# The opening of a two-layer decoder trunk: zeros on TensorE, transfers in another order, the first norm moved

## The chip, the core and the metric

The kernel runs on one core of a Trainium2 chip. The metric is the device time of one execution in microseconds (us). Before the change it is 2430.84 us, the median of 3 runs (2429.31 to 2431.43). The core's engines are TensorE (PE, with PEld for its weight loads), VectorE (DVE), ScalarE (ACT), GpSimd (POOL) and SyncE (SP); here SP issues nearly all DMA transfers.

## What is computed

Two decoder layers over a sequence of 256 positions with a model width of 2048, all in float32, then a last norm. Cut to what matters:

```python
for i in range(2):
    a = rmsnorm(h, attn_norm[i])
    h = h + mixer_i(a)               # q, k, v projection, attention over 16 heads, w_out
    h = h + conv_ffn(rmsnorm(h, ffn_norm[i]), w_up[i], conv_w[i], conv_b[i], w_down[i])
    gate = sigmoid(rmsnorm(h, ple_norm[i]) @ w_ple_gate[i])
    h = h + gate * (p[i] @ w_ple[i])
return rmsnorm(h, final_norm)
```

`p[i] @ w_ple[i]` depends on an input alone. In layer 0 the kernel computes it first of all, before the first projection of the mixer.

## The kernel before

**Tiling.** Activations lie with features on the 128 partitions: `h` is 128 x 16 x 256, feature block by position. All products of weights go through `gemm_unit` (L196). A *unit* is a piece of weights, 128 x (kc blocks of 128 rows) x 256 columns; 4 blocks in most places, 2 for `w_ple`. Every float32 weight piece `wr` is split in two rounded parts: ACT casts the high part (`split_unit`, L165), DVE subtracts it to get the low part (L166). Activations are split likewise into `act` (for the first norm in `norm_parts`, L269 on ACT and L271 on DVE, straight from `h`, since the row factor of the norm is multiplied in behind the product). Three products (high x high, high x low, low x high, `PARTS`) of 128 x 128 by 128 x 256 make up one block, so a unit of 4 blocks is 24 matmuls and one of `w_ple` 12. PE cannot do more than the first two matmuls of a unit before DVE has delivered its low part.

**Order.** The program is written by one Python pass. `tick()` counts units on PE; `defer(n, fn)` puts work n units later. A scheduling layer then fixes one order for each engine. `unit` keeps 3 split units ahead; there are 4 buffers `w` for split weights and 3 buffers `wr` of 8 KB per partition for raw ones. Transfers of weights are *groups*: the first two of 256 KB, then five of 512 KB up to the first w_in pieces, later 1 MB (`_groups`, L90). Below, g0 to g4 are the groups of `w_ple` (8 units), g5 to g8 the four units of the first q product `psq`, g9 and on the units of `psk`; x0 to x3 are the four 512 KB pieces of `h`.

**The opening.** SP issues, in this order, `pr` (the input p), g0, g1, x0, g2, x1, then g3, g4, x2, g5, x3, g6 and the constants `ct`. From g3 on a group has to wait for the split of the group that held its buffer `wr`, and what stands behind it on SP waits as well. POOL issues the gains `gn`, and then `posi`, `bft` and `cv`. PE works through 8 units `psp` (p times w_ple, whose results ACT copies to `pl`), 4 of `psq`, 4 of `psk`, 4 of `psv`, and so on with the next pair of heads. The first norm's sum of squares is made on the way: `norm_squares` (ACT L281, DVE adds to `acc` L282) for all 8 pieces of `h` two units behind the last `psp`, `norm_sums` (four tiny matmuls `nps`, then some 13 operations of two columns on DVE) at 3 units and `norm_rows` (two matmuls `rps`, which give the row factors `rb` and `rq`) at 5 units behind, which is within `psk`.

**Layout.** Pools are allocated in the order `cpool` (h, the activation buffers act0 and act1, pact, pl, constants), `wpool` (wr, w), `work`.

```python
PARTS = ((0, 0), (0, 1), (1, 0))
room = 512 if i < 2 else 1024 if i < 12 else 2048
LOOK = 3
```

Of the kernel before, what the change touches and what calls it, by code (L numbers as in the profile page):

```python
# [17 lines left out]
P = 128  # L18
# [86 lines left out]
def trunk(ctx: ExitStack, tc: tile.TileContext, xT, pT, pos, gains, conv, bf, cst, wst, out):  # L105
    nc = tc.nc

    cpool = ctx.enter_context(tc.tile_pool(name="cpool", bufs=1))
    wpool = ctx.enter_context(tc.tile_pool(name="wpool", bufs=1))
    work = ctx.enter_context(tc.tile_pool(name="work", bufs=1))  # L110
    psum = ctx.enter_context(tc.tile_pool(name="psum", bufs=1, space=bass.MemoryType.PSUM))

    h = cpool.tile([P, KT, S], F32, name="h")
    bufs = [cpool.tile([P, KT, 2, S], F32R, name=f"act{i}") for i in range(2)]
    pact = cpool.tile([P, 2, 2, S], F32R, name="pact")
    pl = cpool.tile([P, KT, S], F32, name="pl")
    gn = cpool.tile([P, 7, KT], F32, name="gn")
    cv = cpool.tile([P, DEPTH, 2 * FT, 4], F32, name="cv")
# [12 lines left out]
    def at_tile(name):  # L131
        return psum.tile([P, 2, 512], F32, name=name, tag="at", bufs=2)
# [11 lines left out]
    def issue_group():  # L144
        g = GROUPS[at["group"]]
        n = sum(u[3] * u[5] for u in g)
        raw = wpool.tile([P, 2048], F32, name="wr", tag="wr", bufs=3)
        src = wst[at["off"]:at["off"] + P * n].rearrange("(p f) -> p f", p=P)
        nc.sync.dma_start(out=raw[:, :n], in_=src)
        at["off"] += P * n  # L150
        at["group"] += 1
        o = 0
        for u in g:
            m = u[3] * u[5]
            raws.append((u, raw[:, o:o + m].rearrange("p (k c) -> p k c", c=u[5])))
            o += m
# [25 lines left out]
    def defer(n, fn):  # L182
        later.append((at["tick"] + n, fn))
# [125 lines left out]
    def norm_rows(mixer):  # L309

        dg = t2_tile("nd", (P, 2, P))
        ps = at_tile("rps")
        for t in range(2):
            nc.vector.tensor_scalar_mul(out=dg[:, t, :], in0=ident, scalar1=rT[:, t:t + 1])
            if mixer is None:
                nc.tensor.matmul(ps[:, 0, t * P:(t + 1) * P], lhsT=ones, rhs=dg[:, t, :],
                                 start=t == 0, stop=True, skip_group_check=True)
        if mixer is None:
            return ps[:, 0, :S]
        dh, dl = t2_tile("ndh", (P, 2, P), F32R), t2_tile("ndl", (P, 2, P), F32R)  # L320
        nc.scalar.copy(out=dh, in_=dg)
        nc.vector.tensor_sub(out=dl, in0=dg, in1=dh.bitcast(F32))
        for i, x in enumerate((dh, dl)):
            nc.tensor.matmul(ps[:, 0, :S], lhsT=trir[:, 0, :], rhs=x, start=i == 0, stop=i == 1)
        nc.vector.tensor_copy(out=rb, in_=ps[:, 0, :S])
        if mixer:
            nc.vector.tensor_scalar_mul(out=rq, in0=rb, scalar1=SCALE)

    def norm_finish(mixer):
        at["rows"] = at["tick"] + 5  # L330
        defer(3, norm_sums)
        defer(5, lambda: norm_rows(mixer))

    def with_rows(fn):

# [14 lines left out]
    def ple_up(l, op):  # L350

        ps = mm_tile("psp")
        gemm(ps, pact, "w_ple", l, op * 256, (2,))
        nc.scalar.copy(out=pl[:, 2 * op:2 * op + 2, :], in_=ps)

    def load_x(i):
        nc.sync.dma_start(out=h[:, 4 * i:4 * i + 4, :], in_=xT[:, 4 * i:4 * i + 4, :])

    nc.gpsimd.dma_start(out=gn, in_=gains)
    praw = load_p(0)  # L360
    issue_group()
    issue_group()
    load_x(0)
    issue_group()
    nc.vector.tensor_copy(out=pact[:, :, 0, :], in_=praw)
    nc.vector.tensor_sub(out=pact[:, :, 1, :], in0=praw, in1=pact[:, :, 0, :].bitcast(F32))
    load_x(1)
    bft = cpool.tile([P, NH], F32, name="bft")
    posi = cpool.tile([32, S], I32, name="posi")
    trir = cpool.tile([P, 2, P], F32R, name="trir")  # L370

    def rest_of_start():
        issue_group()
        issue_group()
        load_x(2)
        issue_group()
        load_x(3)
        issue_group()

    def constants():  # L380
        nc.sync.dma_start(out=ct, in_=cst)
        nc.vector.tensor_copy(out=trir, in_=ct[:, C_ONE:C_ONE + 256].rearrange("p (a b) -> p a b", a=2))
        nc.gpsimd.dma_start(out=posi, in_=pos)
        nc.gpsimd.dma_start(out=bft, in_=bf)
        nc.gpsimd.dma_start(out=cv, in_=conv)


    rc = cpool.tile([32, S], F32, name="rc")
# [179 lines left out]
    def head_pair(l, hp, act, dst, st):  # L568
# [13 lines left out]
        with_rows(lambda ps=ps: nc.vector.tensor_mul(out=q, in0=ps, in1=rq2))  # L582
        ps = mm_tile("psk")
        gemm(ps, act, "w_in", l, D + hp * 256, full)
        nc.vector.tensor_mul(out=k, in0=ps, in1=rb2)

        def first():
            if l % 2 == 0 and hp < 4:
# [10 lines left out]
        if l % 2 == 0 and hp >= 4:  # L599
            rope(q)  # L600
            rope(k)
        defer(2 + (l % 2 == 0 and hp >= 4), first)
        if l % 2 == 1 and hp == 0:
            return
        ps = mm_tile("psv")
# [32 lines left out]
    for l in range(DEPTH):  # L638
        st = {}
        if l == 0:  # L640
            split_unit()
            rest_of_start()
            for op in range(8):
                ple_up(0, op)
            for i in range(8):
                norm_parts(i, 0, X)
            constants()

            def squares():
                for i in range(8):  # L650
                    norm_squares(i)

            defer(2, squares)
            norm_finish(True)
        for hp in range(NH // 2):
            head_pair(l, hp, X, Y, st)
            if l > 0:
# [161 lines left out]
```

## Time and profile before

| | |
|---|---|
| median of 3 runs | 2430.84 us |
| the profiled execution, its own time | 2430.3 us |
| its span, first to last instruction | 2428.5 us |
| mean granted TensorE clock | 0.997 |
| DVE, ACT busy | 66%, 51% of the span |
| moved by DMA | 458.06 MB, mean 189 GB/s |

The 1.8 us between the span and the execution's own time lie outside of all instructions. The profile's page gives busy time and a chain that is followed back from the last instruction; the timeline lists the instructions of one engine in order of time, alike neighbours merged: start, duration, engine, line, operation, written tile <- read tiles, count, and in brackets the idle time ahead and what ended it. The times of a merged row run to the end of the last instruction, so the next row may start before that: instructions overlap at their ends.

### The profile page before, as it was taken

The page shows a single profiled execution, that of the slowest core. Times are in us where ns is not written, and L with a number is a line of the kernel's source. Part 1 is how long each engine was busy: PE and PEld are TensorE (multiplying, and loading weights), DVE is VectorE, ACT ScalarE, POOL GpSimd, SP SyncE. Part 2 cuts the span into 40 slices and gives each one's busy share as a digit, 9 for nine tenths or more (in the row PEclk, how much of TensorE's full clock was granted, in tenths as well). Part 3 has the DMA queues.
Part 4 walks back from the last instruction along what each step waited for, and adds up shares of the span by engine and source line. Part 5 has one row for each costly group of instructions (what it writes and reads, how often), then busy time and mean ns, then how long its engine had stood idle before and what let it go on. Part 6 is the DMA issues. An engine that isn't in the chain of part 4 may idle for free.

```text
span 2428.5 us, 47969 instructions
## 1 busy us (share of the span) xinstructions
PE 2406.8 (99%) x20974; PEld 2400.7 (99%) x20974; DVE 1595.8 (66%) x2157; ACT 1228.6 (51%) x1549; POOL 2.5 (0%) x8
## 2 busy tenths in 40 slices
PE   8999999999999999999999999999999999999997
PEld 8999999999999999999999999999999999999997
DVE  7557666776567657767765555667665776667676
ACT  6554455554355445555554444555544554455553
POOL 0000000000000000000000000000000000000000
PEclk9999999999999999999999999999999999999998
DMA  7444445555555555555455445555555555555553
GB/s 269 174 174 174 170 178 191 192 195 198 197 191 191 187 200 196 197 185 204 176 184 181 170 170 167 199 191 198 193 191 192 193 198 191 201 191 187 193 196 120
DMA packets 66484, 458.06 MB, mean 189 GB/s; under 512 B 7409, under 2 KB 7425, under 8 KB 16609
## 3 DMA queue, kind: packets, MB, share of 16 engines
q1 hardware_dynamic: 66096, 454.53, 53.0%
q8 instruction: 164, 2.69, 0.4%
q0 software_dynamic: 176, 0.46, 0.1%
q14 instruction: 48, 0.39, 0.0%
HBM read 452.86 MB, written 2.10 MB: 187 GB/s over the span
## 4 chain that ended last, share of the span: by engine, by line
PE 98%; DVE 1%; DMA 1%; issue 0%; ACT 0%; SPq 0%; DVEq 0%; ACTq 0%
PE psu L203 39%; PE psd L203 20%; PE pso L203 7%; PE psk L203 7%; PE psq L203 7%; PE psv L237 7%; PE psg L203 7%; DMA wr<-in_w 1%; PE avp L518 1%; PE psp L203 0%; PE pse L717 0%; PE scs L474 0%; PE psv L250 0%; PE sps L509 0%; PE avp L520 0%
## 5 line engine op out<-in xcount | busy, mean ns | idle before, releaser
L166 DVE TENSOR_TENSOR w<-wr,w 128x1024 fp32r<-128x1024 f32 (+2 forms) x882 | 1051.9, 1193 | 694.4 <-ACT w L165 686.8
L165 ACT CAST w<-wr 128x1024 fp32r<-128x1024 f32 (+2 forms) x882 | 905.4, 1028 | 1080.4 <-PE psu L203 353.5
L203 PE MATMUL psu<-act,w 128*128 128x256 f32 x8448 | 959.3, 276 | 0.0
L203 PEld LDWEIGHTS psu<-act,w 128*128 128x128 f32 x8448 | 958.3, 188 | 0.0
L203 PE MATMUL psd<-act,w 128*128 128x256 f32 x4224 | 479.7, 276 | 0.0
L203 PEld LDWEIGHTS psd<-act,w 128*128 128x128 f32 x4224 | 479.2, 188 | 0.0
L203 PE MATMUL psq<-act,w 128*128 128x256 f32 x1536 | 185.7, 280 | 1.2 <-DVE w L166 1.2
L203 PEld LDWEIGHTS psq<-act,w 128*128 128x128 f32 x1536 | 180.3, 188 | 1.8 <-DVE w L166 1.6
L203 PE MATMUL psk<-act,w 128*128 128x256 f32 x1536 | 179.8, 277 | 0.0
L203 PEld LDWEIGHTS psk<-act,w 128*128 128x128 f32 x1536 | 176.5, 188 | 0.0
L203 PE MATMUL pso<-act,w 128*128 128x256 f32 x1536 | 175.8, 277 | 0.0
L203 PEld LDWEIGHTS pso<-act,w 128*128 128x128 f32 x1536 | 174.9, 188 | 0.0
L237 PE MATMUL psv<-w,act 128*128 128x256 f32 x1440 | 173.3, 279 | 0.0
L237 PEld LDWEIGHTS psv<-w,act 128*128 128x128 f32 x1440 | 169.0, 188 | 0.6
L203 PE MATMUL psg<-act,w 128*128 128x256 f32 x1440 | 164.4, 276 | 0.0
L203 PEld LDWEIGHTS psg<-act,w 128*128 128x128 f32 x1440 | 163.7, 188 | 0.0
L617 DVE TENSOR_TENSOR u<-psu,rb 128x512 f32<-128x512 f32 x88 | 60.9, 692 | 33.3 <-PE psu L203 33.2
L623 DVE SCALAR_TENSOR_TENSOR yv<-u,cv,yv 128x256 f32<-128x256 f32 x176 | 73.4, 480 | 0.0
L623 DVE SCALAR_TENSOR_TENSOR yg<-u,cv,yg 128x256 f32<-128x256 f32 x176 | 73.4, 480 | 0.0
L620 ACT ACTIVATE yg<-u,cv 128x256 f32<-128x256 f32 x88 | 48.1, 594 | 1.0 <-DVE u L617 1.0
L620 ACT ACTIVATE yv<-u,cv 128x256 f32<-128x256 f32 x88 | 48.1, 594 | 0.0
L261 ACT CAST act<-yg 128x512 fp32r<-128x512 f32 x44 | 27.4, 622 | 39.2 <-DVE yg L633 39.2
(172 smaller groups left out, 881.7 us busy)
## 6 DMA issues: line engine op xcount, KB each, us to landing
wr<-in_w SPq DMA_DIRECT2D x388, 1024.0 KB, 4.8
wr<-in_w SPq DMA_DIRECT2D x36, 768.0 KB, 4.3
wr<-in_w SPq DMA_DIRECT2D x8, 896.0 KB, 4.7
wr<-in_w SPq DMA_DIRECT2D x7, 512.0 KB, 6.4
h<-in_x SPq DMA_DIRECT2D x4, 512.0 KB, 6.8
out_dram<-h SPq DMA_DIRECT2D x8, 256.0 KB, 2.4
wr<-in_w SPq DMA_DIRECT2D x2, 816.0 KB, 4.4
ct<-in_c SPq DMA_DIRECT2D x1, 841.0 KB, 7.8
```

The lines of the kernel that those rows point to most:

```text
L165: nc.scalar.copy(out=w[:, :, 0, :], in_=raw)
L166: nc.vector.tensor_sub(out=w[:, :, 1, :], in0=raw, in1=w[:, :, 0, :].bitcast(F32))
L203: nc.tensor.matmul(ps[:, j, :], lhsT=w[:, k, s, js], rhs=act[:, k0 - koff + k, t, :], start=first and j + k + n == 0, stop=last and k == k ...
L237: nc.tensor.matmul(ps[:, t], lhsT=act[:, 4 * i + k, a, tsl], rhs=w[:, k, b], start=i + t + k + n == 0, stop=i == 3 and k == kc - 1 and n = ...
L261: nc.scalar.copy(out=dst[:, :, 0, :], in_=src)
L518: nc.tensor.matmul(av[:, 0, j * S:(j + 1) * S], lhsT=v[:, 0, js], rhs=w[:, j * S:(j + 1) * S], start=j == 0, stop=False, skip_group_check= ...
L617: nc.vector.tensor_mul(out=u[:, :, 2:], in0=ps, in1=rb2)
L620: nc.scalar.activation(out=y[:, j, :], in_=u[:, j, 2:], func=AF.Identity, bias=cv[:, l, t, 3:4], scale=cv[:, l, t, 2:3])
L623: nc.vector.scalar_tensor_tensor(out=y[:, j, :], in0=u[:, j, tap:tap + S], scalar=cv[:, l, t, tap:tap + 1], in1=y[:, j, :], op0=ALU.mult, ...
```

## The change

Six things change.

1. PE starts with 20 matmuls of zeros into a PSUM tile `idle` that nobody reads. Their operand is a part of act1 that DVE clears.
2. The raw `w_ple` groups of layer 0 no longer pass through the `wr` buffers; they are loaded into the tile `pl`, each to the place where its own result is written later.
3. SP issues `pr`, g0, g1, g2, x0, g3, x1, g4, x2, g5, g6, x3, g7, `ct`, and then `posi`, `bft` and `cv`, which POOL issued before.
4. The split of `h` (`norm_parts`) is placed between the units of `psp`, and every second copy of a `psp` result goes to DVE.
5. The squares come one piece per unit (3 to 10 units behind the last `psp`, as the program is written), `norm_sums` at 12 and `norm_rows` at 14 units instead of 3 and 5. The products of q and k with the row factors, and the first attention step, wait for that.
6. The pools are allocated with act0, act1, pact and a gap of 64 bytes first, then the weights' buffers, then the rest. From the sizes of the tiles, `w` lies 130,624 bytes behind act0 before and 69,696 bytes behind it now; both are 64 more than a multiple of 512.

```diff
+    apool = ctx.enter_context(tc.tile_pool(name="apool", bufs=1))
+    wpool = ctx.enter_context(tc.tile_pool(name="wpool", bufs=1))
     cpool = ctx.enter_context(tc.tile_pool(name="cpool", bufs=1))
-    wpool = ctx.enter_context(tc.tile_pool(name="wpool", bufs=1))
...
+    bufs = [apool.tile([P, KT, 2, S], F32R, name=f"act{i}") for i in range(2)]
+    pact = apool.tile([P, 2, 2, S], F32R, name="pact")
+    apool.tile([P, 16], F32, name="gap")
     h = cpool.tile([P, KT, S], F32, name="h")
-    bufs = [cpool.tile([P, KT, 2, S], F32R, name=f"act{i}") for i in range(2)]
-    pact = cpool.tile([P, 2, 2, S], F32R, name="pact")
...
-        raw = wpool.tile([P, 2048], F32, name="wr", tag="wr", bufs=3)
+        if g[0][:2] == ("w_ple", 0):
+            op = g[0][4] // 256
+            raw = pl[:, 2 * op:2 * (op + len(g)), :].rearrange("p a s -> p (a s)")
+        else:
+            raw = wpool.tile([P, 2048], F32, name="wr", tag="wr", bufs=3)
...
-    def norm_finish(mixer):
-        at["rows"] = at["tick"] + 5
-        defer(3, norm_sums)
-        defer(5, lambda: norm_rows(mixer))
+    def norm_finish(mixer, sums=3, rows=5):
+        at["rows"] = at["tick"] + rows
+        defer(sums, norm_sums)
+        defer(rows, lambda: norm_rows(mixer))
...
-        nc.scalar.copy(out=pl[:, 2 * op:2 * op + 2, :], in_=ps)
+        if l == 0 and op % 2 == 1:
+            nc.vector.tensor_copy(out=pl[:, 2 * op:2 * op + 2, :], in_=ps)
+        else:
+            nc.scalar.copy(out=pl[:, 2 * op:2 * op + 2, :], in_=ps)
...
+    zero = bufs[1][:, 0, 0, :]
+    nc.vector.memset(zero.bitcast(F32), 0.0)
+    idle = at_tile("idle")
+    for i in range(20):
+        nc.tensor.matmul(idle[:, 0, :S], lhsT=zero[:, 0:P], rhs=zero, start=True, stop=True)
     nc.gpsimd.dma_start(out=gn, in_=gains)
     praw = load_p(0)
-    issue_group()
-    issue_group()
-    load_x(0)
-    issue_group()
+    for _ in range(3):
+        issue_group()
...
-    load_x(1)
...
     def rest_of_start():
+        load_x(0)
         issue_group()
+        load_x(1)
         issue_group()
         load_x(2)
         issue_group()
+        issue_group()
         load_x(3)
         issue_group()
...
-        nc.gpsimd.dma_start(out=posi, in_=pos)
-        nc.gpsimd.dma_start(out=bft, in_=bf)
-        nc.gpsimd.dma_start(out=cv, in_=conv)
+        nc.sync.dma_start(out=posi, in_=pos)
+        nc.sync.dma_start(out=bft, in_=bf)
+        nc.sync.dma_start(out=cv, in_=conv)
...
-        nc.vector.tensor_mul(out=k, in0=ps, in1=rb2)
+        with_rows(lambda ps=ps: nc.vector.tensor_mul(out=k, in0=ps, in1=rb2))
+        late = max(0, at["rows"] - at["tick"])
...
-        defer(2 + (l % 2 == 0 and hp >= 4), first)
+        defer(2 + late + (l % 2 == 0 and hp >= 4), first)
...
             for op in range(8):
+                if op in (2, 4, 6):
+                    for i in (op - 2, op - 1):
+                        norm_parts(i, 0, X)
                 ple_up(0, op)
+            defer(1, lambda: norm_parts(6, 0, X))
+            defer(2, lambda: norm_parts(7, 0, X))
+            constants()
             for i in range(8):
-                norm_parts(i, 0, X)
-            constants()
-            def squares():
-                for i in range(8):
-                    norm_squares(i)
-            defer(2, squares)
-            norm_finish(True)
+                defer(3 + i, lambda i=i: norm_squares(i))
+            norm_finish(True, 12, 14)
```

How the scheduling layer orders this on an engine is not to be read from the diff. On SP, the start before: `pr`, then weights (`wr`) and pieces of `h` in turn, up to the constants.

```order
L347 DMA pr<-in_p 128x512
L149 DMA wr<-in_w 128x512 x2
L357 DMA h<-in_x 128x1024
L149 DMA wr<-in_w 128x1024
L357 DMA h<-in_x 128x1024
L149 DMA wr<-in_w 128x1024 x2
L357 DMA h<-in_x 128x1024
L149 DMA wr<-in_w 128x1024
L357 DMA h<-in_x 128x1024
L149 DMA wr<-in_w 128x1024
L381 DMA ct<-in_c 128x1682
```

And now (line numbers of the changed kernel are higher by 8 to 18):

```order
L157 DMA pl<-in_w 128x512 x2
L157 DMA pl<-in_w 128x1024
L368 DMA h<-in_x 128x1024
L157 DMA pl<-in_w 128x1024
L368 DMA h<-in_x 128x1024
L157 DMA pl<-in_w 128x1024
L368 DMA h<-in_x 128x1024
L157 DMA wr<-in_w 128x1024 x2
L368 DMA h<-in_x 128x1024
L157 DMA wr<-in_w 128x1024
L399 DMA ct<-in_c 128x1682
L401 DMA posi<-in_pos 32x256
```

The first piece of `h` stands behind g2 instead of ahead of it, and all five groups of `w_ple` have a home of their own. On DVE, before, the place from the last parts of `h` to the sum of the squares; `w<-wr,w` is the low part of a unit, `acc<-acc,sq` an addition of squares:

```order
L271 SCALAR_TENSOR_TENSOR act_68<-h,gn,act_68 128x256 x4
L382 CAST trir<-ct 128x256
L282 TENSOR_TENSOR acc<-acc,sq 128x512
L531 CAST sel_13740<-ct 128x16
L282 TENSOR_TENSOR acc<-acc,sq 128x512
L166 TENSOR_TENSOR w<-wr,w 128x4x256
L282 TENSOR_TENSOR acc<-acc,sq 128x512 x2
L166 TENSOR_TENSOR w<-wr,w 128x4x256
L282 TENSOR_TENSOR acc<-acc,sq 128x512 x2
L166 TENSOR_TENSOR w<-wr,w 128x4x256
L282 TENSOR_TENSOR acc<-acc,sq 128x512
```

And the same place now; the three units `w` ahead of the additions are g5, g6 and g7, the one behind them is g8, the last unit of `psq`:

```order
L174 TENSOR_TENSOR w<-wr,w 128x4x256 x2
L363 COPY pl<-psp 128x512
L279 SCALAR_TENSOR_TENSOR act_70<-h,gn,act_70 128x256 x3
L174 TENSOR_TENSOR w<-wr,w 128x4x256
L279 SCALAR_TENSOR_TENSOR act_70<-h,gn,act_70 128x256
L400 CAST trir<-ct 128x256
L290 TENSOR_TENSOR acc<-acc,sq 128x512
L549 CAST sel_13761<-ct 128x16
L290 TENSOR_TENSOR acc<-acc,sq 128x512 x6
L174 TENSOR_TENSOR w<-wr,w 128x4x256
L295 TENSOR_TENSOR acc<-acc 128x256
```

Before, the splits of units stand between the additions; now all seven additions stand ahead of the split of g8. On ACT it is likewise: seven squares in a row between the casts of g7 and g8. On PE, before, from `psp` to the first attention scores `scs`:

```order
L203 MATMUL psp<-pact,w 128x256 x96
L203 MATMUL psq<-act_68,w 128x256 x96
L203 MATMUL psk<-act_68,w 128x256 x12
L291 MATMUL nps<-ct,acc 128x2 x2
L203 MATMUL psk<-act_68,w 128x256 x50
L324 MATMUL rps<-ndh,trir 128x256
L203 MATMUL psk<-act_68,w 128x256 x8
L324 MATMUL rps<-ndl,trir 128x256
L203 MATMUL psk<-act_68,w 128x256 x26
L237 MATMUL psv<-w,act_68 128x256 x48
L428 MATMUL scs<-q,k 128x256 x2
```

And now:

```order
L375 MATMUL idle<-act_71 128x256 x20
L211 MATMUL psp<-pact,w 128x256 x96
L211 MATMUL psq<-act_70,w 128x256 x96
L211 MATMUL psk<-act_70,w 128x256 x96
L245 MATMUL psv<-w,act_70 128x256 x96
L299 MATMUL nps<-ct,acc 128x2 x2
L211 MATMUL psq<-act_70,w 128x256 x48
L332 MATMUL rps<-ndh,trir 128x256
L332 MATMUL rps<-ndl,trir 128x256
L211 MATMUL psq<-act_70,w 128x256 x48
L446 MATMUL scs<-q,k 128x256 x2
```

The norm's matmuls have left `psk` and stand behind `psv` and in the middle of the next pair's `psq`; the first scores follow one unit group later.

## Prediction, made before the changed kernel had run

> **What bounds the kernel now.** First the page: the busy time by engine and the chain that ended last.
>
> ```profile
> PE 2406.8 (99%) x20974; PEld 2400.7 (99%) x20974; DVE 1595.8 (66%) x2157; ACT 1228.6 (51%) x1549; POOL 2.5 (0%) x8
> ...
> PE 98%; DVE 1%; DMA 1%; issue 0%; ACT 0%; SPq 0%; DVEq 0%; ACTq 0%
> ```
>
> PE is the bound; 21.7 us of the span of 2428.5 are without a matmul. A change of the opening can win only what PE loses there, so I look next at PE's timeline, where it starts and where it stops (idle time in brackets), up to the first `psv`.
>
> ```profile
> 5.87 0.80 PE L203 MATMUL psp<-pact,w 128*128 128x256 f32 x2 [5.87 <-ACT w L165]
> 7.42 13.57 PE L203 MATMUL psp<-pact,w 128*128 128x256 f32 x94 [0.76 <-ACT w L165]
> ...
> 24.27 3.31 PE L203 MATMUL psq<-act,w 128*128 128x256 f32 x24 [0.23 <-DVE w L166]
> 28.59 5.50 PE L203 MATMUL psq<-act,w 128*128 128x256 f32 x46 [1.01 <-DVE w L166]
> 33.93 1.52 PE L203 MATMUL psk<-act,w 128*128 128x256 f32 x12
> ...
> 46.65 5.61 PE L237 MATMUL psv<-w,act 128*128 128x256 f32 x48
> ```
>
> The last wait that counts ends at **28.59**: DVE's low part of g7, the third unit of `psq`. From there PE only runs, apart from the norm's matmuls within `psk`. What was lost ahead of 28.59 (the late start, a slow stretch) cannot be won by itself; whatever lets PE be earlier before that point only makes it wait longer there. So the question is what the last such wait of the changed kernel is, and when it ends.
>
> The pace of PE, from the chain of waits in order of time (start, duration) and from windows (length, PE busy, count, granted clock, DMA share, GB/s):
>
> ```profile
> 59.22 8.48 PE psq L203 x72
> 404.76 8.16 PE psu L203 x72
> 1237.40 10.88 PE psk L203 x96
> ...
> 8.00:12.00 4.00, 4.00 (x21) 1.00 1.02 417
> 13.00:17.00 4.00, 4.00 (x36) 1.00 1.01 371
> ```
>
> 8.16/72 and 10.88/96 give 113.3 ns per matmul, the normal pace; 8.48/72 = 117.8 ns is a second one, seen in some stretches around attention. From 8 to 12 us PE is never idle, yet only 21 matmuls fall into 4 us against 36 from 13 to 17: the start runs at about half pace. The 1.00 in the clock's column there says nothing against it; it may be that no change of clock had been recorded yet.
>
> **The change, part by part.** *Zeros.* 20 matmuls at half pace, about 4/20 = 0.2 us each by the window row of 8 to 12, take some 4 us. The first real matmul needs `pr` and g0 and cannot be before 5.87 as now, so zeros that start by 1.8 cost nothing, and what they may save is the slow stretch: the 22 matmuls of the first two units, which now end at about 12 us, would end at 7.4 + 22 x 0.118 = 10.0. By the paragraph above that is worth something only if it moves the last wait.
>
> *Transfers.* Where do the pieces arrive? ACT's timeline, whose first brackets tell the arrival of x0 (8.4) and of g2 (10.44), and which has the durations for what follows; then the transfers' rates by window, and the transfer of `cv` (median us to landing last).
>
> ```profile
> 8.48 1.71 ACT L269 ACTIVATE act<-h,gn 128x256 fp32r<-128x256 f32 x4 [1.12 <-DMA h<-in_x]
> 10.46 1.14 ACT L165 CAST w<-wr 128x512 fp32r<-128x512 f32 x2 [0.27 <-DMA wr<-in_w]
> ...
> 12.50 0.91 ACT L269 ACTIVATE act<-h,gn 128x256 fp32r<-128x256 f32 x2
> 13.31 0.57 ACT L354 COPY pl<-psp 128x512 f32<-128x512 f32 x1
> 13.78 1.15 ACT L165 CAST w<-wr 128x512 fp32r<-128x512 f32 x2
> 14.82 0.59 ACT L354 COPY pl<-psp 128x512 f32<-128x512 f32 x1
> ...
> 18.50 1.05 ACT L165 CAST w<-wr 128x1024 fp32r<-128x1024 f32 x1
> 19.44 0.60 ACT L354 COPY pl<-psp 128x512 f32<-128x512 f32 x1
> ...
> 24.95 1.14 ACT L281 ACTIVATE sq<-h 128x512 f32<-128x512 f32 x2
> 25.99 1.04 ACT L165 CAST w<-wr 128x1024 fp32r<-128x1024 f32 x1
> ...
> 8.00:14.00 6.00, 1.00 1.02 414
> 14.00:24.00 10.00, 1.00 0.99 353
> ...
> cv<-in_conv POOLq DMA_DIRECT2D x1, 352.0 KB, 7.9
> ```
>
> x0 now stands behind g2, so it comes where g2 came, 10.44, less the time of `cv`, which no longer lies in between: 352 KB at 414 GB/s is 0.9 us, nearly all of it ahead of 10.44. I take **x0 at 9.5** (bounds: 8.4, where it was, and 10.44). Behind it each piece of 512 KB takes 1.3 to 1.5 us (414 to 353 GB/s), so x3, the fifth piece after g3, x1, g4, x2, g5, g6, lands at 9.5 + 7 x 1.4 = 19.3 and g7 at 20.7. In the queue of SP the three small transfers now stand ahead of g8: `ct`, 841 KB, `cv`, 352 KB, and g8 take 4.5 to 5 us, so g8 comes at about 25.5.
>
> *ACT.* From x0 on ACT has work without a pause. From start to start: a pair of `act` 0.81 (12.50 to 13.31), a copy 0.47 (13.31 to 13.78), a pair of small casts 1.04 (13.78 to 14.82), a large cast 0.94 (18.50 to 19.44), a square 0.52 (1.04 for two). Up to the end of the cast of g7 stand 8 such pairs, 4 copies (the other 4 are DVE's now), 2 pairs of small casts, 3 large casts and one square: 6.48 + 1.88 + 2.08 + 2.82 + 0.52 = 13.8, with 0.1 for the tail of the last: 9.5 + 13.9 = **23.4**. Of that end the large cast takes 1.05 and four `act` on x3 1.62, so x3 is needed at 20.7 and g7 at 22.3; both have come. So here ACT decides, not the transfers.
>
> *DVE.* Its rows:
>
> ```profile
> 9.03 1.68 DVE L271 SCALAR_TENSOR_TENSOR act<-h,gn,act 128x256 fp32r<-128x256 f32 x4 [0.94 <-ACT act L269]
> ...
> 25.71 0.29 DVE L382 CAST trir<-ct 128x256 fp32r<-128x256 f32 x1
> 25.92 0.69 DVE L282 TENSOR_TENSOR acc<-acc,sq 128x512 f32<-128x512 f32 x1
> 26.52 0.17 DVE L531 CAST sel<-ct 128x16 fp32r<-128x16 f32 x1
> 26.71 0.69 DVE L282 TENSOR_TENSOR acc<-acc,sq 128x512 f32<-128x512 f32 x1
> 27.32 1.22 DVE L166 TENSOR_TENSOR w<-wr,w 128x1024 fp32r<-128x1024 f32 x1
> 28.45 1.48 DVE L282 TENSOR_TENSOR acc<-acc,sq 128x512 f32<-128x512 f32 x2
> ...
> 43.89 0.42 DVE L325 COPY rb<-rps 128x256 f32<-128x256 f32 x1
> ```
>
> Behind the cast of g7 DVE makes its low part (1.13 to the next start, 27.32 to 28.45), one part of `h` (0.40), `trir` (0.21), then seven additions, each of which needs the sum before it: 0.79 from one start to the next (25.92 to 26.71, though a cast of 0.17 lies between; two in a row take 1.48). Only then comes the low part of g8, 1.22. 23.4 + 1.13 + 0.40 + 0.21 + 7 x 0.79 + 1.22 = **31.9**. ACT does the seven squares and the cast of g8 meanwhile: 23.4 + 3.64 + 1.04 = 28.1. So PE waits for DVE, until 31.9. The four copies that DVE takes from ACT are not in the trace; between a copy of half the size, 0.42, and ACT's 0.57, and they fall where DVE waits for ACT anyway. I take them as covered; without that cover the four add up to 2.3 us.
>
> PE, meanwhile: `psq` starts on g5 at about 18.9, has its low part at 20.2, and ends three units at 28.1; two matmuls of the fourth, then idle to 31.9. The remaining 22 take 2.5: `psk` starts at **34.4, against 33.93 now: +0.4**.
>
> *Norm.* `psk` now takes 46.65 - 33.93 = 12.72 for 96 matmuls, which alone take 10.88: the norm's matmuls and the waits for them cost 1.84. They move behind `psv`.
>
> ```profile
> 35.73 0.61 PE L291 MATMUL nps<-ct,acc 128*128 128x2 f32 x4 [0.28 <-DVE acc L287]
> ...
> 41.25 0.16 DVE L306 SCALAR_TENSOR_TENSOR rT<-nt,ny 128x2 f32<-128x2 f32 x1
> 41.45 0.48 DVE L314 TENSOR_SCALAR nd<-ct,rT 128x128 f32<-128x128 f32 x2
> ...
> 42.42 0.39 PE L324 MATMUL rps<-ndh,trir 128*128 128x256 f32 x1 [0.30 <-ACT ndh L321]
> ```
>
> There `nps` costs about 0.5 again, `rps` 0.25. Between them stand 48 matmuls, 5.44 us. From the end of `nps` to `rT` it is 5.1 here (36.3 to 41.4) and to `rps` 6.1, with three splits of 1.2 between DVE's steps; then there will be one, so 5.1 less 2.3, plus 1.0 for `nd` and what ACT does ahead of it, is below the 5.44: the first `rps` does not wait. The second `rps` has another split of 1.2 ahead of its operand, and eight matmuls that lay between the two are gone: a wait of about 0.4 (0 to 1.4). Together 1.2 in place of 1.84: **-0.6**. Behind the later row factors stand q, k and the first scores; from the scores to the next step of attention, `sps`, PE has 120 matmuls as now (96 of `psk` and 24 of `psv` in place of 48 and 72), so nothing more is late.
>
> *Homes.* All matmuls of `psu` run at 113.3 whichever of the buffers they use, so higher bits of an address make no difference in this trace; the low nine bits of the distance between `w` and act0 are the same as before. I cost it at nothing.
>
> Sum: +0.4 - 0.6 = -0.2. The profiled execution took 2430.3, which lies 0.5 below the median of 2430.84: **2430.1 us**, in effect no change.
>
> **Weighing a rule.** The clock in the last microseconds of the program, the only place where a drop of it is recorded, by windows:
>
> ```profile
> 2412.00:2415.30 3.30, 1.74 (x18) 1.00 0.00 0
> 2415.40:2418.40 3.00, 0.36 (x3) 0.50 0.00 0
> ```
>
> After some 3 us with little but tiny matmuls PE's clock is granted at 0.50. PE's pause from 28.6 to 31.9 above is 3.3 us long, the longest in the kernel. The Trainium skill ("TensorE: Matmul & The Clock Gate", section "Why this matters for your kernels") says to leave no pauses of more than about 3 us between bursts of matmuls, since the clock falls back to half after one idle window; this trace agrees at its end, and that speaks against this change. Were the rule to bite here, the sum would be that of the first rival.
>
> **The rivals.** *The clock falls in the pause.* PE then runs at the pace of 8 to 12 us for about as long as it does there, from 7.4 on up to 12.3: 4.9 x (1 - 21/36) = 2.0 us. Against it: the pause is hardly longer than the 3 us seen, and whether the drop comes may depend on where it falls. The same happens if the zeros don't speed up the start: units 0 and 1 end 2 us later, DVE's copies wait for them, and DVE ends its additions up to 2 us later. Either gives 2432.1, both 2434.1: **slower**, from the point where the pause exceeds the 3 us.
>
> *The additions are no obstacle:* if they follow at 0.60 (27.32 less 26.71) or run while DVE would wait, ACT is what is left: 28.1 + 1.2 = 29.3, 2.6 earlier, **2427.5**. For it: DVE does wait for ACT now and then, 0.94 in the row at 9.03. Against it: the seven additions need one another, and the rows show what that takes.
>
> *All waits go:* PE runs through from 7.4: the 192 matmuls of `psp` and `psq` end at 29.2 in place of 33.93, and the norm gives 0.6: 2425.0, **faster by just over 0.2%**. ACT's 13.9 and DVE's 8.5 us would have to shrink by 5 together.
>
> *Pace.* If the new homes, or the order of `idle`, put the matmuls into the 117.8 pace for good, 20,974 x 4.5 ns = 94 us at most; a tenth would decide it. The equal low bits and the uniform `psu` speak against it.
>
> **How the numbers follow.** Forecast 0.45; clock 0.28; no obstacle 0.15; all waits 0.04; pace 0.05 on the slow side, 0.03 on the fast. 8 in 10 lie between 2427.0 and 2433.8. About 0.2%, or 4.9 us, is what a measurement of this kernel tells from no change. Faster 0.06, within 0.2% 0.87, slower 0.07.
>
> **What would show it.** In the changed profile: x0 at 9.5 (ACT's first `act`), the cast of g7 ending at 23.4, seven additions in a row on DVE to 30.7, PE's last long wait ending at 31.9 by the low part of g8, `psk` at 34.4, and `psk` then 10.9 long. If PE's last wait ends before 30, or another engine ends it, the middle of this is wrong; if windows behind it show few matmuls or a clock of 0.5, the first rival holds; another time per matmul in `psu` would refute the whole.

## The result and the profile after

| | before | after |
|---|---|---|
| median time | 2430.31 us (4 runs, 2429.31 to 2431.43) | 2492.97 us (4 runs, 2491.34 to 2493.1) |
| ratio, 95% interval | | 1.0256 [1.0244, 1.0269] |
| the profiled execution, its span | 2430.3, 2428.5 us | 2491.34, 2489.6 us |

The changed kernel is 2.6% slower; 2430.1 us had been forecast. The opening is not where the time went. In the timeline of PE after the change, the same place as in the prediction, `psv` starts at 45.92 where it started at 46.65, and the first `psu` at 403.19 where it started at 404.60:

```profile
19.29 0.40 PE L211 MATMUL psq<-act,w 128*128 128x256 f32 x2
20.64 8.45 PE L211 MATMUL psq<-act,w 128*128 128x256 f32 x72 [0.95 <-DVE w L174]
32.43 2.77 PE L211 MATMUL psq<-act,w 128*128 128x256 f32 x22 [3.34 <-DVE w L174]
35.04 11.04 PE L211 MATMUL psk<-act,w 128*128 128x256 f32 x96
...
403.19 1.52 PE L211 MATMUL psu<-act,w 128*128 128x256 f32 x12
```

So all of the loss lies behind 403 us. There the page's groups tell what grew, in lines of the program that the change doesn't touch (count | busy, mean ns of one from its start to its end, so that neighbours overlap | idle before). Before:

```profile
L203 PE MATMUL psu<-act,w 128*128 128x256 f32 x8448 | 959.3, 276 | 0.0
L203 PE MATMUL psd<-act,w 128*128 128x256 f32 x4224 | 479.7, 276 | 0.0
L203 PE MATMUL psg<-act,w 128*128 128x256 f32 x1440 | 164.4, 276 | 0.0
```

After:

```profile
L211 PE MATMUL psu<-act,w 128*128 128x256 f32 x8448 | 995.8, 281 | 0.0
L211 PE MATMUL psd<-act,w 128*128 128x256 f32 x4224 | 498.5, 281 | 0.0
L211 PE MATMUL psg<-act,w 128*128 128x256 f32 x1440 | 170.4, 281 | 0.0
```

The counts are the same, the idle time is nil in both, and 36.5 + 18.8 + 6.0 = 61.3 us have been added to the busy time: the matmuls themselves take longer. The difference of the two profiled executions is 61.0. A window of 100 us in each layer (length, PE busy and count of matmuls, granted clock, DMA share, GB/s) shows the pace; first before, then after:

```profile
430.00:530.00 100.00, 100.00 (x885) 1.00 0.56 193
1700.00:1800.00 100.00, 100.00 (x885) 1.00 0.54 191
```

```profile
430.00:530.00 100.00, 100.00 (x851) 1.00 0.53 190
1700.00:1800.00 100.00, 100.00 (x851) 1.00 0.52 183
```

PE is busy without a gap in both, at the full clock, with no more DMA traffic than before; it simply does 851 matmuls in the time of 885. These are the two paces that the prediction read from the chain of waits, 113.3 and 117.8 ns from start to start. Counted over the trace from single starts, 1,478 intervals are of 116 to 119 ns before and 15,225 after; 13,747 x 4.45 ns = 61.2 us, the whole loss.

Where does the second pace set in? The timeline of PE at the norm of layer 0's feed-forward part, after the change:

```profile
411.36 0.50 PE L299 MATMUL nps<-ct,acc 128*128 128x2 f32 x4
411.72 5.71 PE L211 MATMUL psu<-act,w 128*128 128x256 f32 x48
417.27 0.28 PE L332 MATMUL rps<-ndh,trir 128*128 128x256 f32 x1
417.45 0.39 PE L332 MATMUL rps<-ndl,trir 128*128 128x256 f32 x1
417.67 4.52 PE L211 MATMUL psu<-act,w 128*128 128x256 f32 x37
```

and the intervals between matmul starts around it, in ns (from the trace, three ahead of `rps`, its two, and what follows):

```
before, rps at  418.67:  113 113 118 | 177 222 | 118 122 116 114 113 114 113 113 114 113 ...
after,  rps at  417.27:  114 113 113 | 184 224 | 117 119 118 118 117 118 118 117 119 117 ...
```

In the changed kernel too `psu` runs at 113 ns up to `rps`. Behind `rps` both kernels stumble for a few matmuls; before, the series falls back to 113 within four, after it stays at 118, and does so for all 6,288 intervals of `psu`, `psd` and the first `psg` up to the next norm, some 740 us. The same happens behind the `rps` at 1164, 1650 and 2397 us; these are the four long stretches. A stretch of 6,288 costs 28.0 us by it, one of `psg` (648, or 552 and the last 95 of `pse`) 2.9.

### The profile page after: what moved, and what is told of

It is laid out like the page before. It is cut to its first block, busy times and chain, and to the rows that moved or that the text cites. A ratio compares the mean times of both kernels' runs of the same rounds, so it can differ in the third digit from the quotient of the medians.

```text
span 2489.6 us, 47999 instructions
## 1 busy us (share of the span) xinstructions
PE 2469.4 (99%) x20994; PEld 2463.4 (99%) x20994; DVE 1598.9 (64%) x2162; ACT 1224.1 (49%) x1544; POOL 0.9 (0%) x5
## 4 chain that ended last, share of the span: by engine, by line
PE 98%; DVE 1%; ACT 1%; DMA 0%; issue 0%; SPq 0%; DVEq 0%; ACTq 0%
PE psu L211 40%; PE psd L211 20%; PE psk L211 7%; PE pso L211 7%; PE psg L211 7%; PE psq L211 7%; PE psv L245 7%; PE avp L536 1%; PE pse L735 0%; PE psp L211 0%; PE scs L492 0%; PE sps L527 0%; PE psv L258 0%; PE avp L538 0%; DMA h<-in_x 0%; ACT act L277 0%
## 5 line engine op out<-in xcount | busy, mean ns | idle before, releaser
L211 PE MATMUL psu<-act,w 128*128 128x256 f32 x8448 | 995.8, 281 | 0.0
L211 PEld LDWEIGHTS psu<-act,w 128*128 128x128 f32 x8448 | 994.7, 189 | 0.0
L211 PE MATMUL psd<-act,w 128*128 128x256 f32 x4224 | 498.5, 281 | 0.0
L211 PEld LDWEIGHTS psd<-act,w 128*128 128x128 f32 x4224 | 497.9, 189 | 0.0
L211 PE MATMUL psg<-act,w 128*128 128x256 f32 x1440 | 170.4, 281 | 0.0
L211 PEld LDWEIGHTS psg<-act,w 128*128 128x128 f32 x1440 | 169.7, 189 | 0.0
```

What stands on the lines that cost most here:

```text
L211: nc.tensor.matmul(ps[:, j, :], lhsT=w[:, k, s, js], rhs=act[:, k0 - koff + k, t, :], start=first and j + k + n == 0, stop=last and k == k ...
```

## The experiments

Three theories to begin with. *Odd* matmuls are here those that are no products of weights, such as `nps` and `rps`. *A:* the buffers' new homes (edit 6) bring the second pace, through the small operands of the odd matmuls ahead of a series, since `w` and act0 kept their distance modulo 512 but everything allocated behind them moved by 64 bytes against them. *B:* the zeros' PSUM tile `idle` (edit 1) moved all later PSUM tiles to other banks; *C:* some lasting effect of the opening's new timing. From the sizes of the tiles in the order of their allocation, these are the places modulo 128 (what is left of the address in bytes after division by 128): act0 lies at 0 and `w` at 64 in both kernels; `trir`, the weights of `rps`, at 0 before and 64 after; `ndh` and `ndl`, its moving operand, at 64 before and 0 after.

All runs in one table, so that the texts below can be short. The four letters are the pace of the four long stretches of the profiled execution, in order of time: `psu` with `psd` of layer 0, `psg` of layer 0, `psu` with `psd` of layer 1, `psg` of layer 1; f is 113.3 ns, s is 117.8 ns, and each stretch is all but a few matmuls of one pace. "rps" gives weights and moving operand modulo 128, behind a semicolon those of the added matmuls. Except for before, after, e23 and e24, each kernel ran once.

| kernel | rps | stretches | us |
|---|---|---|---|
| before | 0, 64 | f f f f | 2430.3 |
| after | 64, 0 | s s s s | 2491.3 |
| e1 after, old homes | 0, 64 | f f f f | 2430.6 |
| e2 before, new homes | 64, 0 | s f s s | 2489.7 |
| e3 after, PSUM banks as before | 64, 0 | s s s s | 2492.8 |
| e4 after, all small tiles 64 on | 0, 64 | f f f s | 2434.3 |
| e5 before, `trir` 64 on | 64, 64 | f f f f | 2430.2 |
| e6 before, `work` 64 on | 0, 0 | f s f s | 2435.2 |
| e7 before, both | 64, 0 | s f s s | 2487.4 |
| e10 old homes, additions on POOL | 0, 64 | f f f f | 2436.4 |
| e15 after, `trir` 64 on | 0, 0 | f f f f | 2432.1 |
| e16 after, `work` 64 on | 64, 64 | f s f f | 2437.0 |
| e17 after, `trir` 32 on | 96, 0 | s f s f | 2488.6 |
| e13 after, one matmul more | 64, 0; then 0, 0 | s s s s | 2494.9 |
| e19 after, as `nps` behind it | 64, 0; then 96, 0 | f f s f | 2462.1 |
| e20 before, two exchanged | 0, 64; then 64, 0 | f s f s | 2437.0 |
| e21 before, two repeated | 0, 64; twice | f f s f | 2459.4 |
| e22 after, two exchanged | 64, 0; then 0, 64 | f f f s | 2435.2 |
| e23 as e1, timed | 0, 64 | f f f f | 2430.3 |
| e24 as e21, timed | 0, 64; twice | f f f s | 2433.6 |

### The homes alone (e1, e2), the PSUM banks (e3), the small tiles (e4)

e1 is the changed kernel with its pools as before:

```diff
-    apool = ctx.enter_context(tc.tile_pool(name="apool", bufs=1))
...
-    bufs = [apool.tile([P, KT, 2, S], F32R, name=f"act{i}") for i in range(2)]
+    bufs = [cpool.tile([P, KT, 2, S], F32R, name=f"act{i}") for i in range(2)]
```

> The changed kernel with edit 6 undone: pools in the order of before, so the small tiles (trir, nd, q, k, v, ct) stand at the addresses of before. Zeros, transfers and norm order stay. Theory A (the pace of the long matmul runs, 113.3 or 117.8 ns, is set by the addresses of the small operands of the odd matmuls ahead of them, rps above all): about 2429, psu at 113.3. Theory B (it is set by the PSUM banks, which the tile idle has moved: mm tiles in banks 4 to 7 in place of 0 to 3): 2493, psu at 117.8. Theory C (it is set by the timing that the new opening leaves): 2493.

e2 is the kernel before with that one edit, the other way round.

> The kernel before with edit 6 alone: new order of the pools with the gap of 64 bytes, opening untouched, PSUM banks as before. Theory A: psu at 117.8, about 2492. Theory B and C: 2430, psu at 113.3.

e3 leaves all of the change and takes the zeros' tile from the other ring of PSUM:

```diff
-    idle = at_tile("idle")
+    idle = mm_tile("idle")
```

> The changed kernel with idle taken from the mm tiles in place of the at tiles, so that mm tiles lie in PSUM banks 0 to 3 again and at tiles in 4 to 7. Theory B: about 2430, psu at 113.3. Theory A and C: 2493, psu at 117.8.

e4 leaves the new order of the pools and puts a gap of 64 bytes ahead of the small tiles:

```diff
     cpool = ctx.enter_context(tc.tile_pool(name="cpool", bufs=1))
...
+    cpool.tile([P, 16], F32, name="gap2")
     h = cpool.tile([P, KT, S], F32, name="h")
```

> The changed kernel with a second gap of 64 bytes ahead of h, so that all small tiles move by 64 bytes against w and act0 (trir at 0 modulo 128, nd, q, k, v at 64, as before the change) while w, act0 and PSUM stay. Theory A: about 2429, psu at 113.3. Theory B and C, and a theory by which the absolute place of w or act0 decides: 2493, psu at 117.8.

Measured: 2430.63, 2489.74, 2492.84 and 2434.29 us. The page's row of `psu` for e1 and for e2:

```profile
L209 PE MATMUL psu<-act,w 128*128 128x256 f32 x8448 | 959.3, 276 | 0.0
```

```profile
L205 PE MATMUL psu<-act,w 128*128 128x256 f32 x8448 | 995.8, 281 | 0.0
```

The homes bring the whole loss, and without them 1.4 us are left (2430.63 against 2429.26), which the eleven executions of e23 below put at 0.4. B falls by e3, C by e1 and e2. e4 says that it is not the order of the pools but 64 bytes of distance: the kernel is back to within 5 us of the 2429.26 of the kernel before beside it, with one `psg` stretch at the second pace (2.9).

### Which operand (e5, e6, e7)

In the kernel before, a gap ahead of `trir` (with one behind it, to leave the rest in place modulo 512), a gap at the start of the pool `work`, and both:

```diff
+    cpool.tile([P, 16], F32, name="gap")
     trir = cpool.tile([P, 2, P], F32R, name="trir")
+    cpool.tile([P, 112], F32, name="gap2")
```

```diff
     work = ctx.enter_context(tc.tile_pool(name="work", bufs=1))
...
+    work.tile([P, 16], F32, name="gap3")
```

> The kernel before with trir alone 64 bytes further on (the weights of the rps matmul); nothing else moves modulo 512. Theory 'the pace of psu is set by the matmuls ahead of it, by where the operands of rps lie': if the weights of rps decide, psu goes to 117.8 ns and the time to 2490 us (2485 to 2493). If the moving operand (ndh, ndl) decides, or if only weights and moving operand together do, psu stays at 113.3 ns and the time at 2429 to 2433.

> The kernel before with all tiles of the pool work 64 bytes further on (ndh and ndl, the moving operand of rps, but also q, k, v and e of the attention); trir, act0 and w stay. If the moving operand of rps decides, psu goes to 117.8 ns and the time to 2490 us (2485 to 2493). If the weights decide, or only both together, psu stays at 113.3 and the time within 2429 to 2437 (the attention's few slow matmuls may change by up to 8 us in either direction).

> Both shifts at once: rps then has its operands as in the kernel after (weights 64, moving operand 0 modulo 128), while act0, w, ct, acc and all of PSUM stay as in the kernel before. By every form of the theory about rps: psu at 117.8 ns, 2490 us (2485 to 2493). If this stays at 2430, the pace is set by something else that moved with the pools (ct, acc, act1, rb), and the theory about rps falls.

Measured: 2430.20, 2435.22 and 2487.43 us. Either shift alone leaves `psu` at 113.3; both together give nearly the whole loss. The windows of e7, a stretch of each kind:

```profile
430.00:530.00 100.00, 100.00 (x851) 1.00 0.52 189
1170.00:1230.00 60.00, 60.00 (x531) 1.00 0.53 186
1700.00:1800.00 100.00, 100.00 (x852) 1.00 0.52 185
```

The middle row is `psg` of layer 0: 60 us/531 = 113.0 ns, while `psu` on both sides of it does 851 and 852 in 100 us. The operands of all three `rps` have the same places, so the places alone don't fix the outcome; in its plain form the theory has a hole here.

### The same from the other side (e15, e16, e17)

The same gaps in the changed kernel, and `trir` by 32 bytes instead of 64.

> The kernel after, with all its new homes, and trir alone 64 bytes further on (a gap ahead of it and one behind, so that nothing else moves modulo 512). Theory: psu falls into its slow pace only where rps has its weights at 64 and its moving operand at 0 modulo 128 together; this takes away the one half, so psu 113.3 ns and 2428 to 2434 us. Rival (the new homes slow psu by something of which the position of trir is only one ingredient): stays at 2485 us or more.

> The kernel after with all tiles of the pool work 64 bytes further on: rps has weights 64 and moving operand 64. Theory as in the run before: psu 113.3 ns; the time 2428 to 2436 us (psg and the attention may keep some of their slow matmuls, as in the run with work alone shifted). Rival: 2485 us or more.

> The kernel after with trir 32 bytes further on instead of 64 (96 modulo 128). If the two places count by halves of 128 bytes, psu stays at 117.8 ns and the time at 2485 to 2493 us; if any distance other than the one of the kernel after breaks it, psu 113.3 ns and 2428 to 2436 us.

Measured: 2432.09, 2436.99, 2488.56 us. One small tile moved by 64 bytes takes 59 us off the changed kernel (2432.09 against its profiled 2491.34); 32 bytes don't. In every trace without added matmuls `psu` is at 117.8 where `rps` has its weights in the upper half of 128 bytes and its moving operand at 0 (five executions, ten stretches of ten), and at 113.3 elsewhere (nine executions, eighteen of eighteen). `psg` does not keep to it.

### Added matmuls, with every buffer in place (e13, e19 to e22)

If the odd matmuls ahead of a series set its pace, others added behind `rps` must change it without moving a buffer. e13 adds one behind each pair, in the changed kernel:

```diff
+        nc.tensor.matmul(ps[:, 1, 0:64], lhsT=ones, rhs=dg[:, 0, 0:64], start=True, stop=True)
         nc.vector.tensor_copy(out=rb, in_=ps[:, 0, :S])
```

> The kernel after with one more small matmul (64 columns, float32, weights from ct, moving operand nd, into the unused half of the bank) directly behind each pair of rps; homes untouched. If the pace of psu is set by the last odd matmul ahead of it and then persists, another one behind rps sets it anew: psu at 113.3 ns and 2430 to 2436 us with the cost of the added matmuls (under 1 us). If instead the new homes slow the psu matmuls as such, or rps counts wherever it stands, psu stays at 117.8 and the time at 2490 to 2495 us.

It stayed slow, 2494.93 us: by what had been expected, a vote against the last odd matmul. Its operands lay at 0 and 0, where `psu` was at 113.3 in e6 and e15, though there with two matmuls of 256 columns in place of one of 64. So e20 and e22 add a pair with weights and moving operand exchanged, e21 repeats `rps` as it is, e19 repeats the form of `nps`:

```diff
+        for x in (dh, dl):
+            nc.tensor.matmul(ps[:, 1, :S], lhsT=x[:, 0, :], rhs=trir, start=True, stop=True)
```

```diff
+        for x in (dh, dl):
+            nc.tensor.matmul(ps[:, 1, :S], lhsT=trir[:, 0, :], rhs=x, start=True, stop=True)
```

```diff
+        for t in range(2):
+            nc.tensor.matmul(ps[:, 1, 0:2], lhsT=acc[:, 0, t * P:(t + 1) * P], rhs=ones[:, 0:2],
+                             start=True, stop=True)
```

> The kernel before with two more matmuls behind each pair of rps, into the unused half of its bank, with weights and moving operand exchanged: weights ndh and ndl (64 modulo 128), moving operand trir (0), the places that rps has in the kernel after. All buffers stay where they were. If the odd matmuls ahead of a long series set its pace by where their operands lie, psu falls to 117.8 ns and the time goes to 2480 to 2492 us, for eight added matmuls. If the pace needs the shifted homes themselves, or rps only sets it when it comes with the homes of the kernel after, psu stays at 113.3 and the time at 2430 to 2434 us.

> The control to the run before: the two added matmuls repeat rps with its own operands (weights trir at 0, moving ndh and ndl at 64). By the theory psu stays at 113.3 ns and the time at 2430 to 2434 us. If it also goes to 2480 or more, it is the number or the timing of the matmuls and not the places of their operands.

> The kernel after with the same two exchanged matmuls: there weights ndh and ndl lie at 0 and the moving operand trir at 64, as rps has them in the kernel before. If the last odd matmuls decide, psu is at 113.3 ns and the time 2430 to 2436 us with all the new homes in place. If one bad pair is enough wherever it stands, or the slow pace once begun isn't undone by other matmuls, 2490 to 2496 us.

> The kernel after with two small matmuls like those of nps (weights acc, two columns of ones) behind each pair of rps, into the unused half of its bank. In the kernel after the stretch of psu between nps and rps runs at 113.3 ns each time, and the stretch behind rps at 117.8. If the last odd matmuls decide, psu 113.3 ns and 2430 to 2437 us; if rps decides wherever it stands, 2490 to 2497 us.

Measured: 2437.00, 2459.42, 2435.16, 2462.10 us. e22 came out as expected: `psu` at 113.3 with all the new homes in place, by its window in layer 0:

```profile
430.00:530.00 100.00, 100.00 (x885) 1.00 0.53 192
```

e19 gave one half of each case. e20 and e21 did not come out as expected. The pair that should have brought the second pace (e20) brought it to `psg` alone, and the control (e21), which should have changed nothing, lost 28 us. Its two windows:

```profile
430.00:530.00 100.00, 100.00 (x885) 1.00 0.52 191
...
1700.00:1800.00 100.00, 100.00 (x852) 1.00 0.52 189
```

By the counts layer 0 is at 113.0 and layer 1 at 117.4 ns, behind the same four matmuls with operands at the same places. So the theory of the places falls as a rule, and what stands is: a series of matmuls can lock into one of two paces when it starts again behind odd matmuls, each change of what runs there (places, number) can tip it, and it then holds until the next odd matmuls. Whether the places act by themselves or through the small shifts of timing that come with them (177 and 222 ns at `rps` before, 184 and 224 after) no run separates.

### Fixed by the program, or by chance? (e23, e24)

> The kernel before with the repeated rps (as e21), where one look had the psu and psd of layer 0 fast and those of layer 1 slow: 2459.4 us. If the pace of a stretch is fixed by the program, every execution is within 2457 to 2462 us. If it falls out anew in each execution, the times are spread over values about 28 us apart: 2431, 2459 and 2487 us.

Ten executions of e24: 2431.10, 2431.23, 2431.88, 2431.89, 2432.72, 2433.62, 2433.89, 2434.08, and 2460.02 and 2461.91 us. With the one of e21, which is the same program, three of eleven lie one stretch of 28 us above the rest. The windows of the profiled execution of e24, at the places of those of e21:

```profile
430.00:530.00 100.00, 100.00 (x885) 1.00 0.55 193
...
1700.00:1800.00 100.00, 100.00 (x885) 1.00 0.53 193
```

The same program does 885 matmuls there in one execution and 852 in another. For this program it falls out anew each time; the program only sets the odds. Those of the kernel before are good for `psu`: each of its 21 executions beside e23 and e24 is between 2429.45 and 2431.01. All four of the kernel after are between 2491.34 and 2493.10. A single execution of another kernel above could have come out otherwise; what carries the reading is that all fourteen without added matmuls agree.

> The kernel after with its homes undone (as e1), timed in five rounds against the kernel before: what the rest of the change, the new opening alone, is worth. The prediction's sum for it was -0.2 us; by the one look at e1, which lost 1.5 us to 15 matmuls at 213 ns behind the pause and gained from fewer slow matmuls in the attention, +0.3 us. Expected: a ratio of 0.9995 to 1.0010 (2429.5 to 2433 us). If the fall of the clock comes in some executions and not in others, the single times differ by about 1.5 us among themselves.

Eleven executions of e23 have a median of 2431.02 us (2429.72 to 2431.70), ratio to the kernel before 1.0002 [0.9993, 1.0011]: without edit 6 the change makes no difference that can be measured.

### The wait of the opening (e10)

e10 has the old homes and makes the seven opening additions on POOL, so that they no longer delay g8:

```diff
-    def norm_squares(op):
+    def norm_squares(op, eng=nc.vector):
...
-            nc.vector.tensor_add(out=acc, in0=acc, in1=sq)
+            eng.tensor_add(out=acc, in0=acc, in1=sq)
...
-                defer(3 + i, lambda i=i: norm_squares(i))
+                defer(3 + i, lambda i=i: norm_squares(i, nc.gpsimd))
```

> The kernel after with the old homes of its buffers (as e1: 2430.6) and the seven opening additions on POOL instead of DVE, so that they no longer stand ahead of the low part of g8. Theory of the opening: the 3.3-us wait of TensorE and the fall of its clock (15 matmuls at 213 ns, 1.5 us) both go, so 2430.6 - 3.3 - 1.5 = 2425.8 us, at least one of the two 2427.3; psu at 113.3 ns. Rival: another wait ends as late (the data of g8 or its cast on ACT behind the seven squares), then 2429 to 2431 us.

Measured: 2436.40, worse, and neither of the two cases. From the timelines of POOL, DVE and PE:

```profile
24.38 10.01 POOL L288 TENSOR_TENSOR acc<-acc,sq 128x512 f32<-128x512 f32 x7 [22.46 <-ACT sq L287]
34.42 0.42 DVE L293 TENSOR_TENSOR acc<-acc 128x256 f32<-128x256 f32 x1 [6.56 <-POOL acc L288]
34.90 1.01 PE L297 MATMUL nps<-ct,acc 128*128 128x2 f32 x4 [5.87 <-DVE acc L293]
```

POOL needs 10 us for the seven, and the scheduling layer put their consumer on DVE ahead of the low part of g8, and `nps` on PE ahead of the last unit of `psq`: DVE stood for 6.56 us, PE for 5.87. PE's clock, too, is granted at 0.50 for 10.24 us, from 31.45 on. The run says nothing on the wait it was to remove, which stays untried in another form. No run made a kernel that beats the one before by more than the measurement can tell.

## Why the prediction was wrong

The step that failed is **Homes**: "All matmuls of `psu` run at 113.3 whichever of the buffers they use, so higher bits of an address make no difference in this trace; the low nine bits of the distance between `w` and act0 are the same as before. I cost it at nothing." What it says of `w` and act0 is true, and in the changed kernel too `psu` runs at 113.3 between `nps` and `rps`. But only the two big operands were weighed. The small tiles moved by 64 bytes against them, and with them the operands of the two `rps` matmuls behind which each long series starts again. e2 puts the price of the term at +60.5 us (2489.74 against 2429.26 of the kernel before on the same chip); e23 shows that nothing else of more than 2.7 us was missed (the upper end of its interval).

The rival **Pace** is what happened, and it was given 0.05 on this side. The sign that was to "refute the whole", another time per matmul in `psu`, is the one that came. Its price, "94 us at most; a tenth would decide it", held: 13,747 of 20,994 matmuls. Its cause was named as "the new homes, or the order of `idle`"; it was the homes (e3). The two arguments against it, equal low bits and a uniform `psu`, looked at the series and not at what sets it off. The evidence was on the table: the prediction quotes 8.48/72 = 117.8 ns "in some stretches around attention", that is, behind odd matmuls.

The other steps:

- *Zeros.* They ran ahead of the data at no cost, and in the kernel after the slow start is gone: the clock is recorded at full from 7.0 us on, before from 12.4. It isn't gone every time: in e13 the clock is granted at 0.50 again from 7.93 to 11.35 us. That the zeros moved no later wait by themselves, as forecast, isn't shown, since no run leaves them out.
- *x0 at 9.5, the cast of g7 at 23.4, additions, end of the wait at 31.9.* ACT's and DVE's timelines:

```profile
9.72 0.51 ACT L277 ACTIVATE act<-h,gn 128x256 fp32r<-128x256 f32 x1 [0.65 <-DMA h<-in_x]
...
22.55 1.04 ACT L173 CAST w<-wr 128x1024 fp32r<-128x1024 f32 x1
```

```profile
25.37 0.69 DVE L290 TENSOR_TENSOR acc<-acc,sq 128x512 f32<-128x512 f32 x1
...
26.16 2.28 DVE L290 TENSOR_TENSOR acc<-acc,sq 128x512 f32<-128x512 f32 x3
28.95 2.29 DVE L290 TENSOR_TENSOR acc<-acc,sq 128x512 f32<-128x512 f32 x3 [0.51 <-DVE acc L290]
31.16 1.22 DVE L174 TENSOR_TENSOR w<-wr,w 128x1024 fp32r<-128x1024 f32 x1
```

  9.72, 23.59, seven additions from 25.37 to 31.2, and PE's wait ends at 32.43: each within 0.6, and the rival "additions no obstacle" is out.
- *`psk`* starts at 35.04, 1.1 later than before (+0.4 forecast), and then runs its 96 in 10.88; `psv` starts 0.73 earlier. The sum of these, with the norm's matmuls further on, was forecast at -0.2; e23 measures a ratio of 1.0002, +0.4 us, with an interval from -1.7 to +2.7. That it is so near is in part luck: the profile of e23 holds 1.3 us lost to the clock (13 matmuls at 213 ns; `psk` starts at 35.91) and 0.7 us won in the attention of layer 0 (725 intervals of 116 to 119 ns in place of 889), and the sum had neither.
- *The clock in the pause.* In the profiled execution of the kernel after the clock held. Windows behind the pause, after and e1:

```profile
32.60:35.80 3.20, 3.20 (x29) 1.00 0.68 236
```

```profile
32.60:35.80 3.20, 3.20 (x17) 0.50 0.85 276
```

  In e1 the clock is granted at 0.50 there, and 15 matmuls take 213 ns each: 15 x 0.1 = 1.5 us, where that rival was given 2.0. Of the eleven profiled executions with this pause (after, e1, e3, e4, e13, e15 to e17, e19, e22, e23) it fell in nine. That it did so as well in the three unprofiled ones of the kernel after, which are 1.6 to 1.8 us above the profiled one, fits but is not shown. The rival holds, then, as a small term; it decided nothing.

## What to carry to other kernels

When an edit moves buffers, don't stop at the operands of the long series: compare the time per matmul, tile by tile, with the profile before, and look at the intervals right behind the odd matmuls that interrupt a series. A loss spread evenly over lines that the edit doesn't touch, at full clock and with no idle time, is a pace and not a wait; a gap of 64 bytes ahead of one small tile is a cheap thing to try, in several executions, since one can mislead. And a control that only repeats what is there is worth its run: here it was the one that overturned the rule.

## What was not expected of the hardware

**Two paces of one matmul.** 128 x 128 by 128 x 256 with its weight load runs at 113.3 or 117.8 ns, at the same granted clock, in blocks of up to 6,288 with hardly one of the other kind between. The Trainium skill ("TensorE: Matmul & The Clock Gate", section "Wait — 56ns, not 53.3ns?") gives the columns over 2.4 GHz plus about 2.5 ns for back-to-back matmuls, by which an estimate for 256 columns is 109.2 ns. The traces show neither that nor a single value, and the measurement decides. Which of the two it is gets settled within seven matmuls behind `rps`, is tipped by shifts of 64 bytes, and can differ between executions of one program (e21, e24). What in PE keeps it, and the rule for the odds, stay open. So do the letters of single `psg` stretches: most kernels were profiled once.

**The clock falls by windows.** In e1 the record of the clock has it rise at 5.26, fall at 32.57 and rise at 35.98 us: 27.31 is eight times 3.413, and 3.41 once more. By the Trainium skill (the same page, section "What's actually happening") the clock is set by free-running windows of 3413 ns, and these rows agree. Laying such windows over each trace, PE was idle for 0.67 to 0.95 of the one that ended at the fall in the nine executions that fell, and for at most 0.53 and 0.49 of one in the two that did not (after, e13). So a pause of 3.0 to 3.4 us, about as long as a window, cost 1.5 us or nothing by where it happened to lie. The idle share alone is no rule: in e13 the clock also fell behind a window idle for 0.54 (4.52 to 7.93 us), hardly more than the 0.53 that did not bring it down, and at the end of the program, among small matmuls, behind one idle for 0.39 (e1, 2411.66 to 2415.07).

**A cast beside POOL.** In e10 DVE's cast of `trir` took 1.39 us while POOL was adding, against 0.29 in the kernel before:

```profile
26.39 1.39 DVE L398 CAST trir<-ct 128x256 fp32r<-128x256 f32 x1
27.70 0.16 DVE L547 CAST sel<-ct 128x16 fp32r<-128x16 f32 x1
```

The smaller cast behind it kept its 0.16. The part of `act` ahead of it, at 24.94, took 1.53 against 0.48 in the kernel after. These are two instructions of one run, and why was not tried.
